# Weight splits of 1024 columns, a heap of 107 tiles and four feed-forward chunks in a two-layer hybrid encoder

## The chip, the cores and the metric

The kernel runs on one core of one Trainium2 chip. The metric is the device time of one execution in microseconds (us). The kernel before took 2399.71 us, the median of three runs (2397.43 to 2399.87). Engines are named as in the profile: PE (TensorE matmul), PEld (its weight load), DVE (VectorE), ACT (ScalarE), POOL (GpSimd) and SP (the engine that issues most DMAs).

## The reference

Two layers over T = 272 tokens (16 learned meta tokens ahead of 256) of width 2048, in float32. Each layer does:

- RMSNorm, then one input projection `p = hn @ w_in`. Its columns feed a latent attention of 8 heads (low-rank queries and keys/values, a shared rotary key, QK-norm, full softmax) and a Hyena group (a width-3 convolution on three streams, `v * x1`, a long bidirectional convolution by FFT with an implicit filter, times `x0`).
- Both groups are normalised, concatenated and go through one output projection, `h = h + mix @ w_out`.
- RMSNorm and a SwiGLU feed-forward, `h = h + (silu(hn @ w_gate) * (hn @ w_up)) @ w_down`, with 5632 = 44 x 128 inner columns.

The meta tokens are dropped at the end, so layer 1 computes 256 columns of tokens from its queries on.

## The kernel before, in words

Features lie on the 128 partitions, tokens along the free axis. Every weight product is `gemm_tile` (line 171): one block of 128 output features, `nk` k-tiles of 128 x 128, all accumulated in one PSUM bank. For float32 accuracy each operand is a sum of two float32r parts, and `mm3` (line 166) issues three matmuls per k-tile: hi by hi, hi by lo, lo by hi (lines 167, 168, 169).

The weights come from HBM whole blocks at a time, up to 2048 columns per partition, into one of `RAW_BUFS` = 3 buffers (`load_raw`, line 139, issued by SP). `Parts` (line 144) splits a block in pieces of `SPLIT_W` = 512 columns. Each piece takes one tile of the pool `hip` and one of `lop`, `SPLIT_BUFS` = 6 of each: ACT copies the piece to hi (line 121), then DVE, or POOL where the piece's number is in the tuple `pool`, computes lo = raw - hi (line 122). A piece is two operands in SBUF for DVE or POOL. The tiles become free when the last matmul that reads them is done. The hi copies stay in program order on ACT, the lo subtractions in program order on DVE, and the weight DMAs in program order on SP (`chain`, line 71); the framework orders everything else at compile time by priority and its own estimate of times.

`sched["uw"]` says which pieces of a Hyena input block `u` POOL splits: (1, 3) in layer 0, two of four, and (1,) in layer 1, one of four. There are 24 such blocks in a layer.

All other SBUF work tiles, 272 float32 wide, come from one pool, `heap`, of `HEAP` = 112 tiles (`HT`, line 88): normalised activations, attention tiles, convolution tables and filters, feed-forward activations.

The order of a layer:

- latents and values (`latent`, the `wv` block);
- `fill` (line 853) emits 24 blocks `u` (line 599, evicted from PSUM by DVE at line 602, then a three-tap convolution at lines 603 to 606) and 16 blocks `wo` of the attention half of the output projection; after each block, `drive` (line 335) moves threads on by one stage: four pairs of heads, the convolution tables (`ftl`, `fr`, `itl`) and four convolution groups (filter parts on DVE and POOL, transforms on PE);
- 16 more `wo` blocks for the Hyena half, with the feed-forward's normalisation alongside;
- the feed-forward (line 876 on). `FF_CHUNKS` (line 22) cuts the 44 inner tiles in chunks of 16, 16 and 12. `gate_up(c)` runs a gate and an up block of 16 k-tiles per inner tile, `down(c)` 16 blocks `wd`, one per output tile, of as many k-tiles as the chunk has, each added to the residual by DVE (line 905). The order is gate_up(0), gate_up(1), down(0), gate_up(2), down(1), down(2).

PSUM has 3 banks for the blocks of `fill` and the feed-forward (`PG`) and 5 for the rest (`PA`).

At the start the first three blocks are loaded and split in quarters of 512 columns (lines 299 to 326), as the residual arrives.

Of the kernel before, what the change touches and what calls it, by code (L numbers as in the profile page):

```python
# [10 lines left out]
F32R = mybir.dt.float32r  # L11
# [4 lines left out]
P = 128  # L16
T = 272
# [3 lines left out]
DFF_T = 44  # L21
FF_CHUNKS = ((0, 16), (16, 16), (32, 12))
HEADS = 8
EPS = 1e-6
SCALE = 192.0 ** -0.5
# [11 lines left out]
RAW_BUFS = 3  # L37
SPLIT_W = 512
SPLIT_BUFS = 6
HEAP = 112  # L40
GB = 3
# [4 lines left out]
SCHED = (  # L46
    dict(lat=1, nets=0, pair=(4, 4, 11, 11), tab=16, conv=(14, 15, 17, 18), gq=1, gp=2, gt=3, gl=1, gw=2, gm=1, gf=3, gk=2, gu=3, gy=2, uw=(1, 3), fe=1),
    dict(lat=0, nets=0, pair=(2, 6, 9, 11), tab=14, conv=(12, 17, 17, 22), gq=2, gp=2, gt=1, gl=1, gw=2, gm=1, gf=1, gk=2, gu=2, gy=2, uw=(1,), fe=1),
)
# [3 lines left out]
def tile_hybrid_encoder(ctx: ExitStack, tc: tile.TileContext, a: dict):  # L53
# [17 lines left out]
    def chain(key, bi):  # L71
        """Keep the instructions of one chain, all on one engine, in the order of the program."""
        if key in CHAINS:
            if key in chains:
                tc.add_manual_dep(
                    bi.ins, chains[key],
                    mybir.DependencyInfo(mybir.DependencyClass.NoSync, mybir.DependencyReason.DATA),
                    reason="stream order")
            chains[key] = bi.ins.name
        return bi  # L80
# [3 lines left out]
    def nm(s):  # L84
        uid[0] += 1
        return f"{s}_{uid[0]}"
# [31 lines left out]
    def split(hi, lo, src, g=None, chained=False, pool=False):  # L118
        """hi + lo = src (times the per-partition gain g), hi with float32r's mantissa."""
        if g is None:  # L120
            h_ = nc.scalar.copy(out=hi, in_=src)  # L121
            l_ = (nc.gpsimd if pool else nc.vector).tensor_tensor(  # L122
                out=lo, in0=src, in1=hi.bitcast(F32), op=ALU.subtract)
            if chained:
                chain("hi", h_)
                if not pool:
                    chain("lo", l_)
        else:
            nc.scalar.activation(hi, src, AF.Copy, scale=g)
            nc.vector.scalar_tensor_tensor(  # L130
                out=lo, in0=src, scalar=g, in1=hi.bitcast(F32), op0=ALU.mult, op1=ALU.subtract
            )
# [11 lines left out]
    class Parts:  # L144
        """Weight columns, split, in tiles of SPLIT_W columns."""

# [8 lines left out]
        def more(self, raw, c, w, pool=False):  # L155
            hi = hip.tile([P, SPLIT_W], F32R, tag="hi", name=nm(self.name + "h"))
            lo = lop.tile([P, SPLIT_W], F32R, tag="lo", name=nm(self.name + "l"))
            split(hi[:, :w], lo[:, :w], raw[:, c : c + w], chained=True, pool=pool)
            self.tiles.append((hi, lo))

# [10 lines left out]
    def gemm_tile(ps, src, nk, xs, t0, name, pool=()):  # L171
        """ps[:, :T-t0] = W block (nk k-tiles of 128 x 128) applied to the split activations xs."""
        parts = Parts(src, nk * P, name, pool)
        for k in range(nk):
            wh, wl = parts.at(k * P)
            xh, xl = xs[k]
            mm3(ps[:, : T - t0], wh, wl, xh[:, t0:T], xl[:, t0:T], k == 0, k == nk - 1)

    def rstd(acc, n, t0, name, more=None):
        """1/sqrt(sum over partitions of acc / n + eps), on every partition."""  # L180
        w = slice(t0, T)
        ps = PA(name + "s")
        MM(ps[:, : T - t0], lhsT=ones, rhs=acc[:, w], start=True, stop=more is None)
        if more is not None:
            MM(ps[:, : T - t0], lhsT=ones, rhs=more[:, w], start=False, stop=True)
        t = HT(name + "r")
        rsqrt(t, HT(name + "r0"), HT(name + "m"), ps[:, : T - t0], w, n)
        return t

    def rsqrt(t, r0, m, psw, w, n):  # L190
        """t[:, w] = 1 / sqrt(psw / n + eps): an estimate and one step of Newton's."""
        nc.scalar.activation(t[:, w], psw, AF.Ln, bias=epsb[:, 0:1], scale=1.0 / n)
        nc.scalar.activation(r0[:, w], t[:, w], AF.Exp, scale=-0.5)
        nc.vector.tensor_scalar(out=m[:, w], in0=psw, scalar1=1.0 / n, scalar2=EPS,
                                op0=ALU.mult, op1=ALU.add)
        nc.scalar.activation(t[:, w], r0[:, w], AF.Square)
        nc.vector.scalar_tensor_tensor(out=t[:, w], in0=t[:, w], scalar=-0.5, in1=m[:, w],
                                       op0=ALU.mult, op1=ALU.mult)
        nc.vector.scalar_tensor_tensor(out=t[:, w], in0=t[:, w], scalar=1.5, in1=r0[:, w],
                                       op0=ALU.add, op1=ALU.mult)  # L200

    class Sum2:
        """Running sum of squares over the feature tiles."""

# [16 lines left out]
    class Normed:  # L221
        """The residual tiles times a gain, split, with the sum of squares alongside."""

# [20 lines left out]

# [1 line left out]
    TWO_PI = 2.0 * math.pi  # L246
# [51 lines left out]

# [1 line left out]
    nx = Normed(0, C_GM, 0, "nm")  # L300
# [34 lines left out]
    def drive(fill, threads):  # L335
        """Emit the tiles of fill; after tile i the threads that start by then move on one stage."""
        live, todo = [], sorted(threads, key=lambda x: x[0])
        i = 0
        done = False
        while not done or live or todo:  # L340
            if not done:
                done = next(fill, "end") == "end"
            while todo and (todo[0][0] <= i or done):
                live.append(todo.pop(0)[1])
            live = [t for t in live if next(t, "end") != "end"]
            i += 1

    for l in range(NL):
# [13 lines left out]

# [1 line left out]
        def w_in(b, t0, name):  # L364
# [29 lines left out]

# [1 line left out]
        SW = ((0, 32), (32, 0), (64, 96), (96, 64))  # L396
# [7 lines left out]
        def rope(src, tabs, t0):  # L404
            """src: [128, T - t0], two groups of 64 rows; the turned tile, with the gain in it."""
            w = slice(t0, T)
# [23 lines left out]

        # values, token-major
        parts = Parts(a["w_v"][l], 2048, "wv")
# [35 lines left out]
        def softmax(ps, n, rk, rq, name):  # L468
            """rq: the columns SCALE / rms of the queries and its negative."""
            mx, sm = SM("mx"), SM("sm")  # L470
# [9 lines left out]
        def pair(pr):  # L480
# [68 lines left out]
            def turn(p):  # L549
                """The probabilities, key-major, split; the last chunk's parts one below the other."""  # L550
                pt = []
# [40 lines left out]

# [1 line left out]
        x0s = [None] * 8  # L594
        vvs = [None] * 8

        def stream_tile(j, b, t0):
            """One 128-channel tile of a projected stream, after the short convolution."""
            ps = w_in(b, t0, "u")
# [21 lines left out]

# [1 line left out]
        sum_y = Sum2("sy")  # L623
# [41 lines left out]

        #   name -> ((table, first column, folded signal), ...), (remainder table, first column)
        FT = {"R0": (((0, 0, 0),), (0, 0)), "R1": (((0, P, 1),), (0, P)),
# [5 lines left out]
        def dft(ps, name, sig, first=True, last_=True):  # L673
            """sig: the signal's sums and differences about its middle, and their remaining rows."""
            main, rem = sig
# [18 lines left out]
        def conv_group(g):  # L694
# [6 lines left out]
            yield from gap("gl")  # L701
            # the filters' sum and difference, token-major, folded about the middle

# [55 lines left out]
            rem_split(brem, rs[1][q0_, :256], slice(0, 256))  # L759
            # the signal, folded  # L760
            folded = []
# [13 lines left out]
            for names in (("R0", "I0"), ("R1", "I1"), ("P",)):  # L775
# [8 lines left out]
                for x, name in enumerate(names):  # L784
                    t = HT("K" + name)
                    nc.scalar.copy(out=t[:, :256], in_=ps[:, x * 256 : (x + 1) * 256])
                    ker[name] = t
            # signal: token-major
            um = [(HT("uh", F32R), HT("ul", F32R)) for _ in range(2)]
# [85 lines left out]

# [1 line left out]
        r2 = nf.rstd()  # L877
# [44 lines left out]
def host_layout(inp):  # L922
# [4 lines left out]
    o = {}  # L927
# [3 lines left out]
    def blocks(w, nk):  # L931
        """[K, M] -> [M/128, 128 (k), K/128 * 128 (m)]"""
        k, m = w.shape
        return np.ascontiguousarray(
            w.reshape(nk, P, m // P, P).transpose(2, 1, 0, 3).reshape(m // P, P, nk * P))
# [79 lines left out]

    # shape-only tables
    pos = np.arange(T, dtype=f)
# [34 lines left out]
    def blocks_of(rows):  # L1052
        """The transform's blocks for the sums and for the differences of the folded signal."""
        c, s_ = C[rows], S[rows]
# [59 lines left out]
```

## Time and profile before

| what | value |
|---|---|
| runs | 2399.71 us median (2397.43, 2399.71, 2399.87) |
| profiled execution: span from first to last instruction | 2399.6 us |
| difference of that span to the median of the runs | 0.1 us |
| PE busy | 2360.7 us (98%), 19026 matmuls |
| DVE / ACT / POOL busy | 1647.8 / 1293.6 / 480.6 us |
| DMA | 402.03 MB, 168 GB/s on average |

The page shows busy time by engine, the span in 40 slices of 60 us with each engine's busy share in tenths, and the clock that TensorE was granted. The windows view gives busy time, number of instructions (x) and granted clock for any stretch. The waits view sums, per engine, the idle time before its instructions and what ended it. The timeline lists instructions in order of start.

### The profile page before, as it was taken

Reading aid. Unit: us, or ns where it says so; the run is one execution under the profiler, and the core shown is the slowest. Engines: PE = TensorE matmul, PEld = TensorE weight load, DVE = VectorE, ACT = ScalarE, POOL = GpSimd, SP = SyncE. Lnnn points to the kernel's source line nnn. Section 1 sums busy time; section 2 is a strip of 40 time slices with the busy share of each in tenths; the row PEclk is TensorE's granted clock in tenths of the full one; section 3 lists DMA queues with packets and bytes.
Section 4 is the critical chain, followed back from the end, with each engine's and each line's share of the span. In section 5 each row is a group of like instructions: output and inputs, shape, how many; then the busy total and the mean of one; then the engine's idle time right before and its main releaser. Section 6 shows DMA issues by size and latency. Waiting matters only on the chain.

```text
span 2399.6 us, 48483 instructions
## 1 busy us (share of the span) xinstructions
PE 2360.7 (98%) x19026; PEld 2338.6 (97%) x19026; DVE 1647.8 (69%) x2997; ACT 1293.6 (54%) x2601; POOL 480.6 (20%) x572
## 2 busy tenths in 40 slices
PE   8999899999999999999999999899999999999999
PEld 7999899999999999999999999899999999999999
DVE  7898998755555555555567899998666655556555
ACT  5777565644444444444456776556455444444443
POOL 3545732211111100110012444432000010000000
PEclk9999999999999999999999999899999999999999
DMA  6434333555555555555554443235555555555554
GB/s 222 157 121 142 122 118 101 198 177 176 176 175 178 174 176 176 176 176 175 166 182 174 146 157 126 91 130 209 181 192 181 188 188 182 193 180 190 187 179 162
DMA packets 72938, 402.03 MB, mean 168 GB/s; under 512 B 8195, under 2 KB 18692, under 8 KB 33156
## 3 DMA queue, kind: packets, MB, share of 16 engines
q1 hardware_dynamic: 72152, 398.38, 48.8%
q8 instruction: 149, 2.44, 0.4%
q14 instruction: 81, 0.66, 0.1%
q10 hardware_dynamic: 556, 0.55, 0.1%
HBM read 396.79 MB, written 2.10 MB: 166 GB/s over the span
## 4 chain that ended last, share of the span: by engine, by line
PE 94%; DVE 4%; issue 1%; ACT 1%; DMA 0%; SPq 0%; DVEq 0%; ACTq 0%
PE fg L168 7%; PE fu L168 7%; PE fg L169 7%; PE fu L169 7%; PE fd L169 7%; PE fd L167 7%; PE fd L168 7%; PE fu L167 7%; PE fg L167 7%; PE u L167 3%; PE u L168 3%; PE u L169 3%; PE wo L167 3%; PE wo L168 3%; PE wo L169 3%
## 5 line engine op out<-in xcount | busy, mean ns | idle before, releaser
L168 PE MATMUL fu<-nfl,wuh 128*128 128x272 f32 (+1 forms) x1408 | 400.5, 284 | 0.0
L168 PE MATMUL fg<-nfl,wgh 128*128 128x272 f32 (+1 forms) x1408 | 400.3, 284 | 0.0
L169 PE MATMUL fu<-nfh,wul 128*128 128x272 f32 (+1 forms) x1408 | 400.0, 284 | 0.0
L169 PE MATMUL fg<-nfh,wgl 128*128 128x272 f32 (+1 forms) x1408 | 400.0, 284 | 0.0
L169 PE MATMUL fd<-ah,wdl 128*128 128x272 f32 (+1 forms) x1408 | 400.0, 284 | 0.0
L167 PE MATMUL fd<-ah,wdh 128*128 128x272 f32 (+1 forms) x1408 | 399.9, 284 | 0.0
L167 PE MATMUL fu<-nfh,wuh 128*128 128x272 f32 (+1 forms) x1408 | 399.8, 284 | 0.0
L168 PE MATMUL fd<-al,wdh 128*128 128x272 f32 (+1 forms) x1408 | 399.7, 284 | 0.0
L167 PE MATMUL fg<-nfh,wgh 128*128 128x272 f32 (+1 forms) x1408 | 399.6, 284 | 0.0
L122 DVE TENSOR_TENSOR wgl<-wg,wgh 128x512 fp32r<-128x512 f32 x352 | 244.5, 695 | 210.9 <-ACT wgh L121 202.7
L122 DVE TENSOR_TENSOR wdl<-wd,wdh 128x512 fp32r<-128x512 f32 x352 | 245.6, 698 | 197.9 <-ACT wdh L121 187.5
L122 DVE TENSOR_TENSOR wul<-wu,wuh 128x512 fp32r<-128x512 f32 x352 | 259.6, 738 | 161.2 <-ACT wuh L121 155.1
L121 ACT CAST wdh<-wd 128x512 fp32r<-128x512 f32 x352 | 218.8, 621 | 280.3 <-PE fd L168 261.0
L121 ACT CAST wgh<-wg 128x512 fp32r<-128x512 f32 x352 | 218.5, 621 | 261.9 <-PE fg L168 141.2
L121 ACT CAST wuh<-wu 128x512 fp32r<-128x512 f32 x352 | 218.6, 621 | 257.5 <-PE fu L168 139.3
L892 POOL TENSOR_TENSOR gt<-gt,up 128x272 f32<-128x272 f32 (+1 forms) x88 | 97.5, 1107 | 1112.3 <-ACT wuh L121 1051.8
L168 PEld LDWEIGHTS fu<-nfl,wuh 128*128 128x128 f32 x1408 | 265.2, 188 | 0.1
L168 PEld LDWEIGHTS fg<-nfl,wgh 128*128 128x128 f32 x1408 | 265.3, 188 | 0.0
L168 PEld LDWEIGHTS fd<-al,wdh 128*128 128x128 f32 x1408 | 265.1, 188 | 0.0
L169 PEld LDWEIGHTS fu<-nfh,wul 128*128 128x128 f32 x1408 | 265.1, 188 | 0.0
L169 PEld LDWEIGHTS fg<-nfh,wgl 128*128 128x128 f32 x1408 | 265.0, 188 | 0.0
L169 PEld LDWEIGHTS fd<-ah,wdl 128*128 128x128 f32 x1408 | 264.9, 188 | 0.0
(373 smaller groups left out, 5885.9 us busy)
## 6 DMA issues: line engine op xcount, KB each, us to landing
wg<-w_gate SPq DMA_DIRECT2D x88, 1024.0 KB
wu<-w_up SPq DMA_DIRECT2D x88, 1024.0 KB
wd<-w_down SPq DMA_DIRECT2D x64, 1024.0 KB
u<-w_in SPq DMA_DIRECT2D x48, 1024.0 KB
wo<-w_out SPq DMA_DIRECT2D x64, 512.0 KB
wd<-w_down SPq DMA_DIRECT2D x32, 768.0 KB
ql<-w_in SPq DMA_DIRECT2D x8, 1024.0 KB
wq<-w_qk SPq DMA_DIRECT2D x8, 1024.0 KB
```

Source lines behind the costliest of these rows:

```text
L121: h_ = nc.scalar.copy(out=hi, in_=src)
L122: l_ = (nc.gpsimd if pool else nc.vector).tensor_tensor(out=lo, in0=src, in1=hi.bitcast(F32), op=ALU.subtract)
L167: MM(ps, lhsT=lh, rhs=rh, start=first, stop=False)
L168: MM(ps, lhsT=lh, rhs=rl, start=False, stop=False)
L169: MM(ps, lhsT=ll, rhs=rh, start=False, stop=last)
L892: nc.gpsimd.tensor_tensor(out=t[:, w], in0=t[:, w], in1=u[:, w], op=ALU.mult)
```

## The change

- `SPLIT_W` is 1024 in place of 512, `SPLIT_BUFS` 5 in place of 6: a block of 2048 columns is two pieces, not four.
- `HEAP` is 107 in place of 112.
- The feed-forward runs in four chunks of 11 inner tiles: gate_up(0), gate_up(1), down(0), gate_up(2), down(1), gate_up(3), down(2), down(3).
- `uw` is (1,) in layer 0, the second of two pieces, so again half of each `u` block is split by POOL; it is () in layer 1, so DVE splits all of it.
- `Parts.more` takes a new tile only where a piece begins one: the quarters of the first three blocks share tiles of 1024, two quarters each.

Comments and docstrings are dropped as well.

```diff
-FF_CHUNKS = ((0, 16), (16, 16), (32, 12))
+FF_CHUNKS = ((0, 11), (11, 11), (22, 11), (33, 11))
...
-SPLIT_W = 512
-SPLIT_BUFS = 6
-HEAP = 112
+SPLIT_W = 1024
+SPLIT_BUFS = 5
+HEAP = 107
...
-    dict(lat=1, ... uw=(1, 3), fe=1),
-    dict(lat=0, ... uw=(1,), fe=1),
+    dict(lat=1, ... uw=(1,), fe=1),
+    dict(lat=0, ... uw=(), fe=1),
...
         def more(self, raw, c, w, pool=False):
-            hi = hip.tile([P, SPLIT_W], F32R, tag="hi", name=nm(self.name + "h"))
-            lo = lop.tile([P, SPLIT_W], F32R, tag="lo", name=nm(self.name + "l"))
-            split(hi[:, :w], lo[:, :w], raw[:, c : c + w], chained=True, pool=pool)
-            self.tiles.append((hi, lo))
+            o = c % SPLIT_W
+            if o == 0:
+                hi = hip.tile([P, SPLIT_W], F32R, tag="hi", name=nm(self.name + "h"))
+                lo = lop.tile([P, SPLIT_W], F32R, tag="lo", name=nm(self.name + "l"))
+                self.tiles.append((hi, lo))
+            hi, lo = self.tiles[-1]
+            split(hi[:, o : o + w], lo[:, o : o + w], raw[:, c : c + w], chained=True, pool=pool)
```

## Rows read from the trace of the kernel before

**Rows 1.** The page: engines, and the span in 40 slices.

```profile
PE 2360.7 (98%) x19026; PEld 2338.6 (97%) x19026; DVE 1647.8 (69%) x2997; ACT 1293.6 (54%) x2601; POOL 480.6 (20%) x572
...
PE   8999899999999999999999999899999999999999
...
DVE  7898998755555555555567899998666655556555
...
PEclk9999999999999999999999999899999999999999
```

**Rows 2.** Windows: span, busy (x count) of PE, PEld, DVE, ACT, POOL, clock, DMA.

```profile
280.00:320.00 40.00, 30.55 (x204) 29.87 (x205) 38.51 (x67) 19.93 (x51) 28.57 (x43) 0.83 0.34 107
1460.00:1540.00 80.00, 67.89 (x494) 65.83 (x493) 72.86 (x138) 45.33 (x121) 43.22 (x74) 0.89 0.29 95
...
540.00:600.00 60.00, 60.00 (x483) 60.00 (x482) 33.89 (x56) 28.48 (x50) 6.60 (x5) 1.00 0.52 176
1800.00:1860.00 60.00, 60.00 (x511) 60.00 (x510) 38.75 (x59) 29.88 (x53) 3.68 (x5) 1.00 0.53 183
```

**Rows 3.** Waits of PE: us in total, times, longest.

```profile
PE u L167 <- DVE u L602: 7.4, 3, 5.5
...
PE wo L167 <- DVE u L602: 3.8, 2, 3.4
PE KR L682 <- DVE ar L692: 3.5, 1, 3.5
PE o L168 <- DVE ptl L564: 3.4, 1, 3.4
...
PE u L167 <- ACT uh L121: 1.7, 2, 0.9
```

**Rows 4.** Timeline, 274 to 285 us: start, us, engine, line, instruction.

```profile
274.62 2.54 DVE L122 TENSOR_TENSOR ftl<-ftw,fth 128x256 fp32r<-128x256 f32 x1
274.70 3.06 POOL L753 TENSOR_TENSOR av<-fb,fb 128x256 f32<-128x256 f32 x4
...
277.09 3.16 DVE L122 TENSOR_TENSOR ul<-u,uh 128x512 fp32r<-128x512 f32 x1
...
278.42 1.28 POOL L122 TENSOR_TENSOR ul<-u,uh 128x512 fp32r<-128x512 f32 x1
...
284.86 0.57 PE L167 MATMUL u<-nmh,uh 128*128 128x272 f32 x1 [5.49 <-DVE u L602]
```

**Rows 5.** Groups by form, DVE, 1040 to 1140 us.

```profile
L122 DVE TENSOR_TENSOR wdl<-wd,wdh 128x512 fp32r<-128x512 f32 x50 | 34.6, 693 | 30.7 <-ACT wdh L121 29.5
...
L905 DVE TENSOR_TENSOR h<-h,fd 128x272 f32<-128x272 f32 x11 | 4.8, 438 | 3.1 <-PE fd L169 3.1
```

**Rows 6.** Groups by form, ACT, 1040 to 1140 us.

```profile
L121 ACT CAST wdh<-wd 128x512 fp32r<-128x512 f32 x50 | 31.1, 622 | 42.0 <-PE fd L168 38.3 <-PE fg L168 1.8 <-PE fu L168 1.8
...
L121 ACT CAST ah<-gt 128x272 fp32r<-128x272 f32 x3 | 1.2, 413 | 0.0
```

**Rows 7.** Groups by form, DVE, 280 to 320 and 1460 to 1540 us.

```profile
L122 DVE TENSOR_TENSOR wol<-wo,woh 128x512 fp32r<-128x512 f32 x10 | 8.4, 853 | 0.1
...
L122 DVE TENSOR_TENSOR wol<-wo,woh 128x512 fp32r<-128x512 f32 x12 | 12.9, 1088 | 1.1 <-ACT woh L121 1.1
```

**Rows 8.** Groups by form, POOL: 40 to 320, 1240 to 1540, 1460 to 1540 us.

```profile
L122 POOL TENSOR_TENSOR ul<-u,uh 128x512 fp32r<-128x512 f32 x48 | 67.1, 1397 | 59.9 <-ACT uh L121 48.3 <-DVE ul L122 5.4 <-PE u L169 4.7
...
L122 POOL TENSOR_TENSOR ul<-u,uh 128x512 fp32r<-128x512 f32 x24 | 33.4, 1391 | 72.3 <-ACT uh L121 58.3 <-DVE knr L197 10.5 <-DVE pth L564 3.3
...
L219 POOL TENSOR_TENSOR saq<-saq,saq 128x256 f32<-128x256 f32 x7 | 5.5, 782 | 8.2 <-ACT saq L215 6.4 <-DMA dec<-dec 1.7
...
L122 POOL TENSOR_TENSOR ul<-u,uh 128x512 fp32r<-128x512 f32 x3 | 4.1, 1357 | 3.7 <-ACT uh L121 3.7
```

**Rows 9.** The chain that ended last: start, us, what.

```profile
27.24 1.24 DVE prel L122
...
147.84 0.60 DVE ul L122
```

More of the change, by code (lines that the diff above doesn't have):

```diff
@@ L46 @@
 SCHED = (
-    dict(lat=1, nets=0, pair=(4, 4, 11, 11), tab=16, conv=(14, 15, 17, 18), gq=1, gp=2, gt=3, gl=1, gw=2, gm=1, gf=3, gk=2, gu=3, gy=2, uw=(1, 3), fe=1),
-    dict(lat=0, nets=0, pair=(2, 6, 9, 11), tab=14, conv=(12, 17, 17, 22), gq=2, gp=2, gt=1, gl=1, gw=2, gm=1, gf=1, gk=2, gu=2, gy=2, uw=(1,), fe=1),
+    dict(lat=1, nets=0, pair=(4, 4, 11, 11), tab=16, conv=(14, 15, 17, 18), gq=1, gp=2, gt=3, gl=1, gw=2, gm=1, gf=3, gk=2, gu=3, gy=2, uw=(1,), fe=1),
+    dict(lat=0, nets=0, pair=(2, 6, 9, 11), tab=14, conv=(12, 17, 17, 22), gq=2, gp=2, gt=1, gl=1, gw=2, gm=1, gf=1, gk=2, gu=2, gy=2, uw=(), fe=1),
 )
```

## The prediction

> **What bounds it now.** I read the page first, then windows, PE's waits, and the timeline around the longest wait. PE is busy 98% of the span, and the slices show where it is not: at the start, in the stretch where layer 0's convolution begins, and around 1440 to 1560 us, layer 1's. There DVE stands at 9 tenths, elsewhere mostly at 5 [rows 1]. So the kernel has two regimes. In the feed-forward PE never pauses, and its pace is 60/483 = 0.1242 us per matmul of 272 tokens and 60/511 = 0.1174 for 256, with DVE busy 33.9 to 38.8 of 60 us [rows 2]. In the two convolution stretches DVE is full (38.5 of 40, 72.9 of 80) and PE waits for it, then runs at a granted clock of 0.83 and 0.89 of the 2.4 GHz level [rows 2]. At the feed-forward's pace 204 matmuls take 25.3 us, so 14.7 of the 40 are lost, 9.45 of them PE's idle time; 494 take 58.0, so 22.0 of 80 are lost, 12.1 of them idle. Each us of DVE's lateness thus costs 14.7/9.45 = 1.55 us in layer 0 and 22.0/12.1 = 1.82 in layer 1, the rest being work at the lower clock.
>
> PE's waits name DVE for evictions (line 602), for attention (564) and for filters (692), hardly for weights: 1.7 us in all go to a late hi copy [rows 3]. So PE waits for what stands behind something in DVE's queue. The timeline shows what: a 256-column subtraction took 2.54 us beside four POOL additions of 3.06 us together, the next 512-column one 3.16 us, and PE's next block waited 5.49 us for an eviction queued behind such work [rows 4]. Alone, 512 columns take 0.69 us [rows 5]. Two operands in SBUF on DVE and an addition on POOL shut each other out.
>
> The profiled span is 2399.6 us, the median of the runs 2399.71, so I sum against 2399.6.
>
> **Feed-forward: nothing.** Matmuls stay the same in number and size. Four chunks add 16 evictions per layer, 32 x 0.44 us [rows 5] = 14 us of DVE, hidden by the 21 to 26 us in 60 that DVE has free [rows 2]. A block `wd` has 33 matmuls, 4.1 us, for 0.69 MB, the bytes per matmul of before. Halving the number of splits saves ACT and DVE time that nobody waits for: a hi copy waits for PE to free a tile [rows 6]. Were that cover gone, 14 us would be the price. The last block still ends in one addition and one store.
>
> **Size of a piece.** Between the 272-column eviction and the 512-column subtraction [rows 5], DVE takes (693 - 438)/240 = 1.06 ns per column, so 1024 columns take 1.24 us against 1.39 for two pieces. Queued pieces start 0.60 us apart [rows 9]; a double one then takes 1.14 against 1.20, a gain of 0.06. ACT: (622 - 413)/240 = 0.87 ns per column [rows 6], 1.07 us against 1.24. PE's first matmul on a piece waits for the whole of it, some 1 us later; five pieces ahead cover that.
>
> **Depth.** Six pieces of 512 are 3072 columns, five of 1024 are 5120: one `u` block more, 48 x 0.124 = 6 us of PE. The two late hi copies go, -1.7 us [rows 3]. In a full stretch, one block's subtractions are already done when it begins: four pieces of 0.60 us in layer 1, 2.4 us, two in layer 0, 1.2 us. The bounds are nothing, if the compile-time order spends the lead elsewhere, and all of it. I take all, since DVE has room ahead of both stretches [rows 1].
>
> **Fewer turns at the lock.** In the stretches 10 and 12 `wo` pieces took 853 and 1088 ns [rows 7] against 693: 1.6 and 4.7 us lost to POOL. Half as many pieces queue half as often, saving between 0 and 0.8 in layer 0, 0 and 2.4 in layer 1; what POOL has to do stays, so I take half, 0.4 and 1.2. The 0.06 us saved per pair gives 0.3 (5 pairs) and 0.8 (13 pairs, the `u` pieces too).
>
> **POOL's share in layer 1.** 24 pieces, 33.4 us, leave POOL [rows 8]; DVE gets 24 x 0.60 = 14.4 us more over 200 us. In the full stretch it is 3 pieces: +1.8 us on DVE, against 4.1 us of POOL [rows 8] that shut DVE out for between 0 and 4.1. I take these as equal: 0, with ends of +1.8 and -2.3.
>
> **POOL's share in layer 0.** It keeps half the columns (48 pieces, 67.1 us [rows 8]) in pieces twice as long. By 0.77 us for 256 columns and 1.28 for 512 [rows 4], 2.0 ns per column, a piece of 1024 holds POOL 2.3 us, 1.0 more. With about two of them in the full stretch, that is between 0 and +2.1; I take +1.0. The rows show DVE waiting through a run of four POOL additions, not for one [rows 4]: if POOL keeps its turn while it has work, only the sum of its columns counts, and the length of a piece nothing, which is the lower end. The Trainium skill (SBUF — State Buffer, "Who interferes with whom") says that the loser blocks until the instruction that went first has finished. By it alone a wait would grow with the piece and the term would be +2.1; the 3.16 us that one DVE piece took speak for more than one instruction's wait.
>
> **Small terms.** The first three blocks need six tiles of 1024 where five exist, so the last one's copy waits for PE: between 0 and one copy and one subtraction, 0.62 + 1.24 [rows 6, 9]; as the start waits for data anyway, +0.5. The heap has five tiles less, which no row prices; convolution loads would be issued later, and POOL waited 1.7 us for one [rows 8]. Between 0 and 1.7 per layer; I take +0.5 together.
>
> **Sum.** Layer 0: -1.2 - 0.3 - 0.4 + 1.0 = -0.9, times 1.55 = -1.4. Layer 1: -2.4 - 0.8 - 1.2 = -4.4, times 1.82 = -8.0. The rest: -1.7 + 0.5 + 0.5 = -0.7. Together -10.1: 2389.5 us. Good ends throughout give -2.3 x 1.55 - 7.9 x 1.82 - 1.7 = -19.6, 2380; bad ends +2.1 x 1.55 + 1.8 x 1.82 + 1.9 + 3.4 = +11.8, 2411.
>
> **Rivals.**
> - *Only the order changes.* The total of DVE and POOL work in the full stretches is nearly the same, and the new order puts other work ahead of the same evictions: the depth gives nothing there, nor the lock. Layer 0 then has +1.0 x 1.55, the rest -0.7: 2400.5. For it: weights are hardly what PE waits for [rows 3]. Against it: DVE has room before both stretches.
> - *POOL's long pieces, in layer 0, slower.* From the slice that begins at 180 us on DVE stands at 8 tenths or more [rows 1]; say half of the 24 long pieces fall where it has no room, and each holds it for the full 1.0 us more: 12 x 1.0 x 1.55 = +18.6, in place of the +1.6 in the sum, makes 2406.5. It decides from (4.8 + 11.7)/(12 x 1.55) = 0.9 us per piece on. For it: 2.54 and 3.16 us in rows 4. Against it: half as many turns, and runs of POOL additions that do the same already.
> - *The stalls mostly go.* If the order also puts line 602 ahead of the table splits, the 5.5 us wait [rows 3] goes as a whole, 8.5 us at 1.55: 2381.
>
> **How the numbers follow.** The forecast has 0.42, its own range being 2382 to 2395. The large gain has 0.08, only the order 0.28, POOL's long pieces 0.22. A measurement of this kernel tells 0.2%, 4.8 us, from no change. So faster has 0.50, same 0.28, slower 0.22. The range of 2377 to 2408 takes in the forecast and two rivals with some of the spread of their terms, and leaves out about a tenth at either end.
>
> **What would show it.** In the changed profile PE keeps 483 and 511 matmuls per 60 us in the feed-forward; DVE splits of 1024 take 1.24 us and ACT's 1.07; PE waits for no hi copy; layer 1's convolution stretch shows more matmuls and a higher clock than 0.89, with DVE still near full. POOL `u` pieces of 2.3 us in layer 0 with DVE pieces well over 2.5 us beside them, and an idle time over 9.45 us there, would make the slower rival right. Fewer matmuls per slice in the feed-forward, or waits at new places (loads, the start), would make it all wrong.

## The result and the profile after

The changed kernel takes 2423.53 us (median of 4 runs, 2422.66 to 2424.89), the kernel before beside it 2399.38 (4 runs): ratio 1.0098, 95% interval [1.0085, 1.0110]. It is slower by about 23.5 us, where 10 us less was forecast, and 15.5 us beyond the upper end of the range. The profiled span is 2423.1 us.

The page, as [rows 1] shows it of before:

```profile
PE 2365.6 (98%) x19026; PEld 2342.3 (97%) x19026; DVE 1584.6 (65%) x2427; ACT 1182.8 (49%) x1951; POOL 425.8 (18%) x524
...
PE   7999989999999999999999998899999999999999
...
DVE  7788897855555555555676888888555555555554
```

The same matmuls, and 63.2 us less busy time on DVE, 110.8 on ACT, 54.8 on POOL: three engines do less, and the time is longer. The windows say where (columns as in [rows 2]: us, PE, PEld, DVE, ACT, POOL busy, clock, DMA share, GB/s). The first line of the first fence and the line of the second are the same piece of the program, layer 1 from its first `kv` matmul to its first gate matmul, after and before; the other lines are of the changed kernel:

```profile
1253.80:1671.50 417.70, 396.08 (x3133) 388.46 (x3132) 346.98 (x662) 250.66 (x525) 130.80 (x181) 0.98 0.42 142
...
240.00:300.00 60.00, 54.48 (x411) 52.17 (x410) 54.54 (x108) 32.29 (x67) 37.95 (x36) 0.94 0.46 152
300.00:360.00 60.00, 52.95 (x391) 51.68 (x389) 54.04 (x114) 35.95 (x92) 28.92 (x59) 0.91 0.28 87
540.00:600.00 60.00, 60.00 (x481) 60.00 (x480) 31.66 (x35) 24.73 (x30) 3.87 (x5) 1.00 0.51 175
1500.00:1560.00 60.00, 48.78 (x354) 46.76 (x353) 50.72 (x96) 29.53 (x74) 27.61 (x53) 0.89 0.28 90
1800.00:1860.00 60.00, 60.00 (x510) 60.00 (x509) 32.89 (x37) 26.15 (x32) 3.73 (x5) 1.00 0.55 182
```

```profile
1241.40:1648.80 407.40, 394.32 (x3132) 388.09 (x3131) 354.82 (x745) 264.94 (x631) 155.45 (x206) 0.98 0.43 145
```

The feed-forward keeps its pace: 481 and 510 matmuls per 60 us, against 483 and 511 in [rows 2]. Layer 1's piece takes 10.3 us longer for the same matmuls (the counts differ by one that lies across an edge). PE is idle in it (span less busy time) for 21.6 us in place of 13.1, while DVE is busy 7.8 us less. So DVE's amount of work is not what PE waits for there. The waits of PE (us in total, times, longest), as in [rows 3]:

```profile
PE u L170 <- DVE u L605: 11.8, 3, 5.4
PE pre L170 <- ACT preh L121: 7.4, 2, 6.4
PE KR L171 <- DVE kl L122: 4.9, 1, 4.9
...
PE KR L685 <- DVE ar L695: 3.8, 2, 2.6
PE pt L559 <- DVE p L480: 3.0, 1, 3.0
```

Line 605 is the eviction of `u` (602 before, 7.4 us there). The blocks `u` and `wo` wait for no hi copy any more, only the start does; PE waits for more of the small work that stands in DVE's queue.

From here on every run is told by four lengths of its profiled execution, worked out from the trace: *mixer 0* is from the start of the span to layer 0's first gate matmul (448.3 us before), *feed-forward 0* from there to layer 1's first `kv` matmul (793.1), *mixer 1* to layer 1's first gate matmul (407.4), *end* the rest. For the changed kernel they are longer by 10.5, 2.1, 10.4 and 0.6 us. The lengths are of one execution each; executions of one kernel lie up to 8 us apart (2405.60 to 2413.27 us with ten tiles of 512), so a change of a few us in one of the lengths is not exact.

### The profile page after: what moved, and what is told of

The parts are those of the page before. It is cut to its first block, busy times and chain, and to the rows that moved or that the text cites. A ratio compares the mean times of both kernels' runs of the same rounds, so it can differ in the third digit from the quotient of the medians.

```text
span 2423.1 us, 46534 instructions
## 1 busy us (share of the span) xinstructions
PE 2365.6 (98%) x19026; PEld 2342.3 (97%) x19026; DVE 1584.6 (65%) x2427; ACT 1182.8 (49%) x1951; POOL 425.8 (18%) x524
## 3 DMA queue, kind: packets, MB, share of 16 engines
q8 instruction: 150, 2.46, 0.4%
## 4 chain that ended last, share of the span: by engine, by line
PE 83%; DVE 3%; issue 1%; ACT 1%; POOL 0%; DMA 0%; SPq 0%; DVEq 0%; ACTq 0%; POOLq 0%
PE fd L171 7%; PE fu L171 7%; PE fg L171 7%; PE fu L172 7%; PE fg L172 7%; PE fd L172 7%; PE fg L170 7%; PE fu L170 7%; PE fd L170 7%; PE wo L170 2%; PE wo L171 2%; PE wo L172 2%; PE u L170 2%; PE u L171 2%; PE u L172 2%
## 5 line engine op out<-in xcount | busy, mean ns | idle before, releaser
L122 DVE TENSOR_TENSOR wdl<-wd,wdh 128x1024 fp32r<-128x1024 f32 (+1 forms) x256 | 230.6, 901 | 199.7 <-ACT wdh L121 199.7
L121 ACT CAST wdh<-wd 128x1024 fp32r<-128x1024 f32 (+1 forms) x256 | 200.1, 782 | 320.4 <-PE fd L171 240.6
L122 DVE TENSOR_TENSOR wul<-wu,wuh 128x1024 fp32r<-128x1024 f32 x176 | 215.8, 1226 | 186.2 <-ACT wuh L121 184.7
L122 DVE TENSOR_TENSOR wgl<-wg,wgh 128x1024 fp32r<-128x1024 f32 x176 | 231.0, 1312 | 142.7 <-ACT wgh L121 139.1
L121 ACT CAST wuh<-wu 128x1024 fp32r<-128x1024 f32 x176 | 184.8, 1050 | 283.2 <-PE fg L171 147.3
L121 ACT CAST wgh<-wg 128x1024 fp32r<-128x1024 f32 x176 | 184.7, 1049 | 239.7 <-PE fu L171 139.9
L895 POOL TENSOR_TENSOR gt<-gt,up 128x272 f32<-128x272 f32 (+1 forms) x88 | 66.5, 756 | 1213.3 <-DVE up L894 1192.3
L170 PEld LDWEIGHTS fu<-nfh,wuh 128*128 128x128 f32 x1408 | 265.5, 189 | 0.0
L170 PEld LDWEIGHTS fg<-nfh,wgh 128*128 128x128 f32 x1408 | 265.5, 189 | 0.0
L170 PEld LDWEIGHTS fd<-ah,wdh 128*128 128x128 f32 x1408 | 265.4, 188 | 0.0
```

The lines of the kernel that those rows point to most:

```text
L122: l_ = (nc.gpsimd if pool else nc.vector).tensor_tensor(out=lo, in0=src, in1=hi.bitcast(F32), op=ALU.subtract)
L170: MM(ps, lhsT=lh, rhs=rh, start=first, stop=False)
L895: nc.gpsimd.tensor_tensor(out=t[:, w], in0=t[:, w], in1=u[:, w], op=ALU.mult)
```

## The experiments

**The small parts, one by one.** Three runs make one part of the change in the kernel before.

```diff
-HEAP = 112
+HEAP = 107
```

> The kernel before with a heap of 107 tiles and nothing else. Theory 'long pieces' (POOL's and DVE's pieces of 1024 columns make the loss) expects 2399 us, within 5. Theory 'heap' (five tiles less delay loads and convolution work) expects most of the 24 us: 2412 to 2424, lost before 460 us and between 1440 and 1660 us. Theory 'order' (any edit makes the compile-time order anew, and the two convolution stretches come out better or worse by chance) expects a move of 5 to 15 us of either sign in those stretches alone.

Measured 2402.37 us against 2400.57, ratio 1.0012 [1.0002, 1.0021]; mixers +0.6 and -3.4, feed-forward 0 +3.5.

```diff
-FF_CHUNKS = ((0, 16), (16, 16), (32, 12))
+FF_CHUNKS = ((0, 11), (11, 11), (22, 11), (33, 11))
```

> The kernel before with four feed-forward chunks of 11. All theories expect the feed-forward's pace unchanged, 0.124 and 0.117 us per matmul, and 2398 to 2402 us. Layer 0's mixer is emitted ahead of the chunks, so it should be the same to 1 us. A loss over 4 us in the feed-forward would put part of the 24 us on the chunks.

Measured 2402.63 us, 1.0012 [1.0003, 1.0022]; mixers -1.4 and -0.3.

```diff
-    dict(lat=0, ... uw=(1,), fe=1),
+    dict(lat=0, ... uw=(), fe=1),
```

> The kernel before with all of layer 1's u blocks split by DVE (pieces of 512). Theory 'long pieces' expects layer 1's mixer within 4 us of before, so 2396 to 2404. A theory 'DVE load' (layer 1 loses its 10 us because DVE takes 24 x 0.60 us more) expects 2408 to 2414, all of it after 1300 us. 'Order' expects a move in layer 1's convolution stretch of either sign.

Measured 2398.71 us, 0.9994 [0.9984, 1.0003]; mixers -1.9 and -0.4. None of the three comes near 23 us. The spread of the mixers, where such a part should do nothing, is up to 3.4 us; it is put down here to the new compile-time order, which no run shows by itself.

**The size of a piece taken back, the depth kept.** The changed kernel with ten tiles of 512 (and POOL's pieces of before):

```diff
-SPLIT_W = 1024
-SPLIT_BUFS = 5
+SPLIT_W = 512
+SPLIT_BUFS = 10
...
```

> The changed kernel with its pieces back at 512 columns, ten tiles of each part (the same bytes and the same depth of 5120 columns), u pieces shared with POOL as before; heap of 107 and chunks of 11 stay. Theory 'long pieces' expects the 24 us back: 2394 to 2402, and no DVE instruction held for 2 us by one POOL instruction. 'Heap' expects 2412 to 2424 still. 'Order' expects anything between 2390 and 2425, with gains and losses in the convolution stretches alone.

Measured 2409.69 us, 1.0037 [1.0024, 1.0050]; mixers +4.9 and +3.9. More than half of the loss goes with the size.

**Size alone and depth alone in the kernel before.** Four tiles of 1024 with heap and chunks of before, `uw` as in the change; then eight of 512, without POOL's pieces in layer 1:

```diff
-SPLIT_W = 512
-SPLIT_BUFS = 6
+SPLIT_W = 1024
+SPLIT_BUFS = 4
...
```

> The changed kernel with four tiles of 1024 columns (depth 4096), and with the heap of 112 and the three feed-forward chunks of before: what is left of the change is the width of the pieces, a smaller step in depth, and the sharing with POOL. Theory 'width' (pieces of 1024 on POOL and DVE hold the other engine longer and make the loss) expects 2412 to 2424 still, with DVE instructions of 256 to 272 columns held for 2 us and more beside one POOL instruction in layer 0. Theory 'depth' (splits taken further ahead push other work back on DVE and ACT) expects about half of the 24 us, 2406 to 2414. 'Order' expects no rule.

```diff
-SPLIT_BUFS = 6
+SPLIT_BUFS = 8
...
```

> The kernel before with eight tiles of 512 columns (depth 4096 again) and layer 1's u pieces all on DVE, which by itself left the time as it was. The partner of the kernel with four tiles of 1024: same depth, same sharing of columns, half the width. 'Width' expects 2394 to 2402, and the difference between the two to be 10 us or more; 'depth' expects 2404 to 2410 and both kernels to be alike within 4 us.

The first measured 2430.07 us against 2401.12, 1.0122 [1.0107, 1.0137], mixers +17.1 and +7.5: the larger piece costs even more when there are fewer of them. The second measured 2402.76, 1.0006 [0.9997, 1.0015], mixers +4.9 and -3.1: with pieces of 512, more lead gains nothing.

**POOL's long pieces in layer 0.** The changed kernel without them, so that DVE splits all of `u`:

```diff
-    dict(lat=1, ... uw=(1,), fe=1),
+    dict(lat=1, ... uw=(), fe=1),
```

> The changed kernel with POOL's u pieces of layer 0 taken over by DVE: no subtraction of 1024 columns is left on POOL. If POOL's long pieces cost layer 0 its 8.5 us between 60 and 460 us, layer 0's feed-forward begins 5 to 9 us earlier and the time is 2414 to 2419. A theory 'DVE load' expects layer 0 to lose more, 24 x 1.14 us more on DVE: 2428 or above. Layer 1 should stay as it is, with its 7.27 us DVE instruction.

Measured 2414.81 us, 1.0055 [1.0038, 1.0072], 10.3 us less than with them (1.0098 less 1.0055). Mixer 0 is +4.9 in place of +10.5, so 5.6 us of it were POOL's. Mixer 1, whose program is the same, is +7.2 in place of +10.4; the last section shows one long wait of DVE beside POOL that the changed kernel has there and this run has not. One such place in the timeline (start, us, engine, line, instruction); first the changed kernel, then the one with instructions of 512 columns that comes next:

```profile
219.55 2.40 POOL L122 TENSOR_TENSOR ul<-u,uh 128x1024 fp32r<-128x1024 f32 x1 [4.39 <-ACT uh L121]
219.78 2.46 DVE L200 SCALAR_TENSOR_TENSOR knr<-knr,knm 128x272 f32<-128x272 f32 x1 [0.47 <-ACT knr L199]
```

```profile
218.68 1.36 POOL L122 TENSOR_TENSOR ul<-u,uh 128x512 fp32r<-128x512 f32 x1 [3.06 <-ACT uh L121]
218.81 1.53 DVE L200 SCALAR_TENSOR_TENSOR knr<-knr,knm 128x272 f32<-128x272 f32 x1
```

A DVE instruction of 0.43 us took as long as POOL's one piece beside it, 2.46 or 1.53 us: 0.93 us more for the long one. The changed kernel's mixer 0 has 14 DVE instructions that take over 2 us beside one or two POOL instructions, from 84 to 283 us. At 0.93 us each that is an estimated 13 us of DVE, of which the end of mixer 0 sees 5.6.

**The length of an instruction, with tiles of 1024 kept.** Copies and subtractions both made in instructions of 512; then only the subtractions; then only the copies:

```diff
...
-            for c in range(0, ncols, SPLIT_W):
-                self.more(raw, c, min(SPLIT_W, ncols - c), c // SPLIT_W in pool)
+            for c in range(0, ncols, 512):
+                self.more(raw, c, min(512, ncols - c), c // 512 in pool)
```

> The changed kernel with its tiles of 1024 columns kept, but filled by two instructions of 512 on ACT and two on DVE or POOL. Theory 'instruction length' (it is the single 1.2 us DVE and 2.4 us POOL instruction that makes other work late) expects both mixers to come back to what ten tiles of 512 gave: 2402 to 2412, layer 0's feed-forward begun by 454 us, and no 2 us hold by one POOL instruction. Theory 'tile size' (a tile of 1024 is freed and ready only as a whole, so splits come in bursts) expects 2418 to 2426 still.

(`uw` counts pieces of 512 there: (1, 3), half of each block as before.) Measured 2414.50 us against 2401.33, 1.0059 [1.0044, 1.0074]; mixers +5.1 and +2.9.

```diff
...
-            split(hi[:, o : o + w], lo[:, o : o + w], raw[:, c : c + w], chained=True, pool=pool)
+            chain("hi", nc.scalar.copy(out=hi[:, o : o + w], in_=raw[:, c : c + w]))
+            for s in range(0, w, 512):
...
```

> The changed kernel with hi copies of 1024 on ACT and the subtractions in two instructions of 512. If the length on DVE and POOL is the cause, it does as well as the kernel that halves both, within 4 us. If ACT's copies of 1.07 us make attention and convolution work late, it stays near the changed kernel, 2416 to 2426.

Measured 2422.05 us, 1.0090 [1.0073, 1.0107]; mixers +7.3 and +9.7.

```diff
-            split(hi[:, o : o + w], lo[:, o : o + w], raw[:, c : c + w], chained=True, pool=pool)
+            for s in range(0, w, 512):
+                e = min(s + 512, w)
+                chain("hi", nc.scalar.copy(out=hi[:, o + s : o + e], in_=raw[:, c + s : c + e]))
+            l_ = (nc.gpsimd if pool else nc.vector).tensor_tensor(
+                out=lo[:, o : o + w], in0=raw[:, c : c + w],
+                in1=hi[:, o : o + w].bitcast(F32), op=ALU.subtract)
...
```

> The changed kernel with ACT's copy of a piece made as two copies of 512 columns; DVE's and POOL's subtraction stays one of 1024. If the length of ACT's copy is what layer 1's mixer pays for (the run with short instructions throughout +2.9, the one with short subtractions and a long copy +9.7): layer 1's mixer +2 to +4, layer 0's +9 to +11 as POOL's long pieces stay, 2414 to 2418. If the subtraction's length is what costs there: layer 1's mixer stays at +9 to +11, 2421 to 2425. If both of them count for half: +6, 2419.

Measured 2429.93 us against 2400.69, 1.0122 [1.0107, 1.0137]; mixers +11.6 and +11.8. The reading that ACT's long copy is what layer 1 pays for has fallen: with short copies it is as bad, and the whole kernel is worse. In mixer 1 either of the two being long costs as much as both (+9.7 and +11.8 against +10.4). What the two have in common, as I read it, is the wait between them: one subtraction of 1024 can't begin before two copies are done, and two subtractions of 512 can't begin before one long copy is. Only where both are short does a piece's first half go to DVE while ACT does the second. DVE's groups by form in 1260 to 1660 us agree in the idle time ahead of the `u` subtractions (busy us, mean ns | idle before them, and what ended it), one fence each for short and short, long and long, and short copies with a long subtraction:

```profile
L122 DVE TENSOR_TENSOR ul<-u,uh 128x512 fp32r<-128x512 f32 x96 | 69.5, 752 | 10.8 <-ACT uh L121 10.5
```

```profile
L122 DVE TENSOR_TENSOR ul<-u,uh 128x1024 fp32r<-128x1024 f32 x48 | 63.5, 1325 | 17.4 <-ACT uh L121 17.2
```

```profile
L165 DVE TENSOR_TENSOR ul<-u,uh 128x1024 fp32r<-128x1024 f32 x48 | 61.0, 1273 | 25.6 <-ACT uh L164 25.3
```

DVE stands still for the copy 10.5, 17.2 and 25.3 us. The subtractions keep the program's order, so DVE can't do what stands behind one meanwhile.

**Depth alone, at tiles of 1024.** Three tiles, 3072 columns as in the kernel before, in place of five; once with short instructions, once with the long ones:

```diff
-SPLIT_BUFS = 5
+SPLIT_BUFS = 3
```

> The changed kernel with tiles of 1024 but copies and subtractions of 512 columns, as in the run with short instructions (2414.5), now with three tiles in place of five: 3072 columns of lead, as in the kernel before. Depth theory: the lead of 5120 columns itself moves weight work ahead of evictions, which is what all runs with 4096 or 5120 columns of lead share, +4.9 us in layer 0's mixer; with 3072 it goes back to within 1.5 of before, and the time to 2402 to 2407. Length theory (only the length of instructions costs): nothing changes, 2412 to 2417, layer 0's mixer +5. Order theory (any new schedule costs some us at either place): a number for neither, layer 0's mixer anywhere from -3 to +5.

> The changed kernel with three tiles of 1024 in place of five, copies and subtractions of 1024 columns kept. Depth theory plus length: layer 0's mixer +5 to +6 in place of +10.5 (POOL's long pieces stay), layer 1's mixer +7 in place of +10.4, 2414 to 2418. Length theory alone: unchanged, 2421 to 2425. Too little lead (a copy of 1024 columns waits for PE to free one of three tiles, and PE waits for it): PE's waits name the hi copies, the feed-forward falls below 481 matmuls per 60 us and the time is over 2428.

Measured 2422.12 us, 1.0090 [1.0075, 1.0105], and 2433.10 us, 1.0138 [1.0121, 1.0155], against 2400.69. Mixers +9.4 and +10.0, and +18.5 and +15.1. The depth theory has fallen the other way round: fewer tiles are worse by 7.4 and 9.6 us (1.0090 less 1.0059 and 1.0138 less 1.0098, of 2400).

**The tile's size alone.** The last run left the same 3072 columns and the same instructions of 512, in six tiles in place of three, with the change's heap, chunks and `uw` in layer 1:

```diff
-SPLIT_W = 1024
-SPLIT_BUFS = 5
+SPLIT_W = 512
+SPLIT_BUFS = 6
...
-    dict(lat=1, ... uw=(1,), fe=1),
+    dict(lat=1, ... uw=(1, 3), fe=1),
```

> The changed kernel with SPLIT_W 512 and six tiles, and the same columns on POOL in layer 0 (pieces 1 and 3): heap of 107 tiles, four chunks and no POOL piece in layer 1 stay. It differs from the run with short instructions and three tiles of 1024 (2422.1) by nothing but the tile's size, at the same 3072 columns. Tile-size theory (a tile of 1024 frees and refills its columns at once, so that two subtractions stand in a row on DVE ahead of an eviction, whatever the length of an instruction): 2398 to 2405, both mixers within 3 us of the kernel before, uninterrupted stretches of weight subtractions on DVE of 0.85 to 0.95 us on average against 1.03 to 1.23. Sum theory (the three parts that cost nothing alone cost something together): 2412 to 2424.

Measured 2404.45 us against 2400.30, 1.0017 [1.0008, 1.0026]; mixers +0.7 and -0.1, feed-forward 0 +3.5. So three tiles of 1024 in place of six of 512, at the same columns and instructions, cost 17.5 us (1.0090 less 1.0017); the size of a tile and the number of tiles change together here. With three, the start is longer by 2.3 us (last `pre` matmul at 37.3 us against 35.0), and PE waits 3.0 us for hi copies of `u` against 1.1. With the three runs it makes a path from the kernel before to the changed one:

```
step                                                ratio     us of 2400   mixer 0   mixer 1
six tiles of 512, all other parts of the change     1.0017       +4.1       +0.7      -0.1
three tiles of 1024, instructions of 512            1.0090      +17.5       +8.7     +10.1
five tiles of 1024, instructions of 512             1.0059       -7.4       -4.3      -7.1
five tiles of 1024, instructions of 1024 (changed)  1.0098       +9.4       +5.4      +7.5
sum                                                             +23.5      +10.5     +10.4
```

Each ratio is known to 2 to 4 us on either side, so a step of the table to 4 or 5 us, and how the loss is shared among the steps depends on the path. By way of the ten tiles of 512 (1.0037) it is +4.1, then +4.8 for the lead, +5.3 for tiles of 1024 at the same 5120 columns and short instructions (1.0059 less 1.0037, with intervals that overlap), and the same +9.4. The mixers of these two runs with 5120 columns are alike, +4.9 and +3.9 against +5.1 and +2.9, though the profiled execution of the first took 2413.27 us, above its median of 2409.69, and that of the second 2412.58, below its 2414.50. So a cost of the tile's size is clear with three tiles and not with five. What holds on either path: +10.1 us from six tiles of 512 to five of 1024, and +9.4 for instructions of 1024 on them, POOL's long pieces in layer 0 among these. With three tiles the long instructions cost 11.5 us (1.0138 less 1.0090), 5.1 of it in mixer 1.

What a larger tile does is inferred, and the runs do not tell whether it acts in the queues or through the order made at compile time. As I read it, its columns come free at once, when the 24 matmuls on it are done, and are refilled at once, and two subtractions stand in a row on DVE. From layer 1's first `u` matmul to the first gate, the weight subtractions that follow one another on DVE with nothing between them make stretches of 0.88 us on average before and 0.84 with six tiles of 512; with tiles of 1024 they are 1.14 (five) and 1.23 (three) with short instructions, 1.37 in the changed kernel. They do not go in step with the loss: 1.46 where only the copies are long (mixer 1 +9.7), 1.34 with three tiles and long instructions (+15.1). DVE's idle time ahead of the `u` subtractions, by the same row as above:

```profile
L122 DVE TENSOR_TENSOR ul<-u,uh 128x512 fp32r<-128x512 f32 x96 | 71.6, 751 | 9.8 <-ACT uh L121 8.7
```

```profile
L122 DVE TENSOR_TENSOR ul<-u,uh 128x512 fp32r<-128x512 f32 x96 | 70.8, 766 | 13.9 <-ACT uh L121 13.1
```

The first is of six tiles of 512, the second of three of 1024: 8.7 and 13.1 us, with the same instructions. Over the runs with all of layer 1's `u` on DVE, this wait and mixer 1 go up together, though not in step: 8.4 to 10.0 us of wait with tiles of 512 (-3.1 to -0.1 us of mixer), 10.5 and 13.1 with short instructions in tiles of 1024 (+2.9, +10.0), 16.5 to 18.3 where a long copy is in it (+7.2 to +15.1), 25.3 with two copies ahead of a long subtraction (+11.8).

What such a delay does to PE is on the changed kernel's chain of waits, 1520 to 1540 us (start, us, what):

```profile
1525.29 1.73 POOL yp L827
...
1527.07 0.29 issue
1527.36 1.05 ACT woh L121
...
1528.43 1.22 DVE wol L122
1529.65 0.34 DVE yl L122
1529.99 1.32 DVE fb L735 x4
```

A weight's copy and subtraction, 2.27 us, stand on the chain between a product of the convolution on POOL and the next steps of the convolution on DVE (`yl`, `fb`), which are behind them in DVE's queue.

**POOL left out of the weights, and the lock measured by itself.** The kernel before with `uw` empty in both layers:

> The kernel before with all u pieces of both layers on DVE, 512 columns each. DVE gets 48 x 0.60 = 29 us more in layer 0 and is rid of POOL's 67 us of subtractions that shut it out. If DVE's own time sets layer 0's mixer, 2403 to 2415; if the time shut out does, 2390 to 2400, which would be the best version of all. Layer 1 as in the run with that change alone, 0 to -2 us.

Measured 2402.43 us, 1.0006 [0.9996, 1.0015]: with pieces of 512, POOL's share is worth nothing that can be told from the noise.

Two kernels that only time DVE beside a run of n POOL additions, first with one tile for all of them, then with a tile each:

> Computes none of the reference: one DVE instruction of 256 columns is released by a POOL addition, behind which POOL has n = 0, 1, 2, 4, 8, 14 more additions of 256 columns ready, three kinds of DVE instruction in turn (two operands in SBUF; the same with a per-partition scalar; one operand in PSUM and one in SBUF). If POOL keeps its turn as long as it has work, the first two kinds take 0.42 + 0.7 n us, up to 10 us, and the third 0.42 always. If the loser waits for one instruction only, they take at most 1.2 us for every n. A share of turns between the two expects 0.42 + 0.7 us from n = 1 on, and POOL's next addition delayed.

> Computes none of the reference: as the first measurement of a DVE instruction beside n ready POOL additions, but these write n different tiles, so that each can start before the one ahead of it has ended (in the first measurement they started 0.80 us apart and took 0.72, a pause in which DVE got in). If POOL keeps its turn while its instructions overlap, the two kinds of DVE instruction with two operands in SBUF take 0.42 + 0.7 n us, up to 10 us at n = 14. If the loser waits for one instruction, 1.2 us at most for every n. The third kind, with one operand in PSUM, 0.42 us.

They took 93.14 and 84.70 us. In the first one's timeline (start, us; n is the count of POOL instructions that follow):

```profile
36.09 1.05 DVE L89 SCALAR_TENSOR_TENSOR dstt<-gstt,par,y 128x256 f32<-128x256 f32 x1 [0.84 <-POOL gstt L81]
36.14 0.72 POOL L84 TENSOR_TENSOR qstt<-gstt,y 128x256 f32<-128x256 f32 x1
...
51.42 1.05 DVE L89 SCALAR_TENSOR_TENSOR dstt<-gstt,par,y 128x256 f32<-128x256 f32 x1 [6.11 <-POOL gstt L81]
51.47 11.20 POOL L84 TENSOR_TENSOR qstt<-gstt,y 128x256 f32<-128x256 f32 x14
```

With one POOL addition behind it or 14, DVE takes 1.05 us, 0.48 alone: it waits for one instruction and then has its turn, although its row starts 0.05 us ahead of POOL's. `tensor_tensor` took 0.43 every time, and so did the one with an operand in PSUM. The other tile layout changed none of this.

## Why the prediction was wrong, point by point

- **"What bounds it now"** failed first. PE's waits for DVE were read as a lack of DVE's time, and DVE's 9 tenths as full. After the change DVE is busy 7.8 us less in layer 1's mixer, and PE is idle 8.5 us more. And 24 or 72 more subtractions on DVE, with as many off POOL, cost nothing (`uw` empty in layer 1 0.9994, in both 1.0006). What the runs point to is how long a small instruction stands behind something in DVE's queue, and that grew. The factors 1.55 and 1.82, which turn DVE work into time, had nothing to stand on: by the trace the mixers got 10.5 and 10.4 us longer for 9.7 and 8.5 us of added idle time of PE, 1.1 and 1.2.
- **Size of a piece.** The durations were right: 1.24 us forecast and 1.23 to 1.33 measured on DVE, 1.07 and 1.05 on ACT. The groups by form in 1040 to 1140 us, as [rows 5, 6] of before:

```profile
L122 DVE TENSOR_TENSOR wul<-wu,wuh 128x1024 fp32r<-128x1024 f32 x12 | 14.7, 1226 | 14.1 <-ACT wuh L121 14.1
L122 DVE TENSOR_TENSOR wgl<-wg,wgh 128x1024 fp32r<-128x1024 f32 x11 | 14.6, 1330 | 10.0 <-ACT wgh L121 10.0
...
L121 ACT CAST wuh<-wu 128x1024 fp32r<-128x1024 f32 x12 | 12.6, 1051 | 21.6 <-PE fg L171 11.7 <-PE fu L171 9.8
```

  What failed is "five pieces ahead cover that". The five pieces cover the matmuls on the weights, and PE indeed waits for none of them; they don't cover what stands behind a piece on DVE. The term was -0.06 us per pair; it is +9.4 for the instruction's length, in which POOL's long pieces are counted too, and for the tile's size +17.5 at 3072 columns and +5.3, not clear of the noise, at 5120. For the size the sum had no term at all.
- **Depth.** The term, with its factors and the two late copies, was -1.2 x 1.55 - 2.4 x 1.82 - 1.7 = -7.9 us, and at tiles of 1024 two tiles more give 7.4 or 9.6. But it was counted in columns, as if six tiles of 512 and three of 1024 were the same. With pieces of 512, ten tiles against six cost 4.8 us (1.0037 less 1.0017; POOL's piece in layer 1 differs too). From six tiles of 512 to five of 1024, with short instructions, the measured step is +10.1 us where this term promised -7.9.
- **Fewer turns at the lock.** Right for the `wo` pieces, and too small: in layer 1's stretch, 1440 to 1560 us, they took 1256 ns (first row below), no more than the 1226 to 1330 of the feed-forward, against 1088 over 693 before in 1460 to 1540 [rows 7]. But the wait went elsewhere: line 607 of the convolution took 1437 ns there (second row), by one instruction of 7.27 us among its eight, where the same line of before, 604, took 840 (third row).

```profile
L122 DVE TENSOR_TENSOR wol<-wo,woh 128x1024 fp32r<-128x1024 f32 x7 | 8.8, 1256 | 0.6 <-ACT woh L121 0.5
...
L607 DVE SCALAR_TENSOR_TENSOR uc<-u,par,uc 128x257 f32<-128x257 f32 x8 | 11.5, 1437 | 4.5 <-ACT uc L606 4.5
...
L604 DVE SCALAR_TENSOR_TENSOR uc<-u,par,uc 128x257 f32<-128x257 f32 x8 | 6.7, 840 | 2.5 <-ACT uc L603 2.5
```

- **POOL's share in layer 1: nothing.** Right (0.9994, with pieces of 512).
- **POOL's share in layer 0.** +1.0 x 1.55 = +1.6 us was forecast, of ends from 0 to +2.1 x 1.55 = +3.3; it is 5.6 in mixer 0, and 10.3 in the whole kernel, 3.2 of it in mixer 1. The price per place, 1.0 us, was right (0.93). The Trainium skill (SBUF — State Buffer, "Who interferes with whom") says that whoever comes second waits for the whole of the instruction that went first. The trace agrees, with 2.46 us beside one piece of 2.40. The kernels made for it agree in the length of the wait, 1.05 us whatever the count, though there DVE's row is the first by 0.05 us. What was mis-sized is the number of places: they were sought in the full stretch of 280 to 320 us alone, two, where the trace has one there and 13 ahead of it. The rival's count, 12, was nearly right; but it let each of them delay the end by 1.55 times its length, 18.6 us in all, and what they cost mixer 0 together is less than half of their length.
- **Feed-forward, start, heap.** Four chunks cost 0.7 to 5.3 us (1.0012 [1.0003, 1.0022]) where "nothing" was forecast. The heap alone cost 0.5 to 5.0 us (1.0012 [1.0002, 1.0021]), near its ends of 0 to 3.4, but by luck: late convolution loads were the reason given, and the loss stands in the pace of feed-forward 0 (+3.5), with mixer 1 shorter by 3.4. The start lost 1.9 us up to the last `pre` matmul, the upper end. Heap, chunks and layer 1's POOL pieces together measured +4.1 us.
- **The rivals.** None named what happened. "Only the order changes" came nearest in its reason (other work ahead of the same evictions), but gave the order no price. The slower rival's 2406.5 us was passed by 17 us, most of it by other ways.

## What to carry to other kernels

An engine that is busy nine tenths and is waited for isn't yet a bound by its work: ask which instruction PE waits for, and what stands ahead of it in that queue. There, as far as this kernel shows, tiles and instructions of background work should be short enough that urgent work isn't held up, even where long ones cost less in total, and the lead is to be bought by more tiles of the same size, if at all. When two sizes change at once, count the lead in tiles that can come free one by one, not in columns.

## What the runs showed of the hardware that was not expected

- One DVE instruction of about 0.49 us took 7.27 us in the changed kernel, and the timeline has POOL busy without a pause beside it; DVE's row first, then POOL's:

```profile
1538.15 7.27 DVE L607 SCALAR_TENSOR_TENSOR uc<-u,par,uc 128x257 f32<-128x257 f32 x1 [0.67 <-ACT uc L606]
...
1538.06 0.73 POOL L750 TENSOR_TENSOR rt<-rt,ru 18x256 f32<-18x256 f32 x1
1538.76 0.73 POOL L748 TENSOR_TENSOR rt<-rt,skip 18x256 f32<-18x256 f32 x1
...
1543.47 1.66 POOL L769 TENSOR_TENSOR vf<-uc 128x128 f32<-128x128 f32 x4
```

  Sixteen POOL instructions passed in that time. The rule of the Trainium skill (SBUF — State Buffer, "Who interferes with whom") and the kernels made for it give a wait for one. The run with ten tiles of 512 has the same wait, 7.26 us. In the changed kernel it stands on the chain of waits that leads to PE's next convolution matmuls (start, us, what):

```profile
1538.15 7.27 DVE uc L607
1545.42 0.10 DVE kl L122
```

  So a part of that kernel's +10.4 us in mixer 1 can be this one wait; the run without POOL's pieces in layer 0, with the same program in layer 1 and without the wait, is +7.2. It is not the whole cause, as runs without it lose up to 15.1 us there. What lets POOL keep its turn in one place and not in the other is open; the phase at which DVE arrives was not varied.
- The feed-forward's pace changes with nothing but the heap's size: feed-forward 0 has 6336 matmuls in 793.1 us before, 125.2 ns each, and 796.6 us, 125.7 ns, with the heap of 107 alone. The same heap with six and ten tiles of 512 has 796.5 and 796.8, but with tiles of 1024 793.6 to 795.1. In 540 to 600 us it is 480 matmuls against 483 [rows 2], PE never pausing in either (the line is of six tiles of 512):

```profile
540.00:600.00 60.00, 60.00 (x480) 60.00 (x478) 33.73 (x55) 28.51 (x50) 6.62 (x5) 1.00 0.52 176
```

  The runs leave its cause open, as they do the +4.9 us that mixer 0 shows in the three runs with eight or ten tiles of 512 or without POOL's long pieces, and how much of a mixer's change up to 3.6 us is order alone.
